# A backbone of three token mixers: all two-operand passes moved to VectorE, and a decay buffer of its own in the state-space stage

## The chip, the cores and the metric

The kernel runs on one core of one Trainium2 chip. The metric is the device time of one execution in microseconds (us). The engines are named as the profile names them: PE is TensorE (matmuls, with PEld for its weight loads), DVE is VectorE, ACT is ScalarE, POOL is GpSimd and SP is SyncE, which issues every DMA of this kernel.

## The reference, cut to what matters

Two layers over 256 context and 512 latent tokens of 1024 channels, all in float32. Each layer normalises and modulates the tokens, projects them into the inputs of three mixers, and projects the mixers' joined outputs back:

```python
for l in range(DEPTH):                      # DEPTH = 2
    u_lat = rmsnorm(h_lat, norm_w[l]) * (1.0 + scale[:, None]) + shift[:, None]
    ...
    ssd_c, ssd_l = ssd_branch(...)          # state space, 16 heads, chunks of 128 tokens
    gla_c, gla_l = gla_branch(...)          # gated linear attention, 4 heads, chunks of 64
    s5_c, s5_l = s5_branch(...)             # diagonal complex scan, 32 groups
    out_lat = jnp.concatenate([ssd_l, gla_l, s5_l], axis=-1) @ w_out[l]
    h_lat = h_lat + gate[:, None] * out_lat
return rmsnorm(h_lat, final_norm_w)
```

The state-space branch is the one that the change rewrites. With `acs` the running sum of the step sizes times a negative rate, it computes in each direction and chunk

```python
acs = jnp.cumsum(da, axis=-1)
decay = jnp.exp(segsum(da))                 # exp(acs[t] - acs[s]) for s <= t, else 0
cb = jnp.einsum("bclgn,bcsgn->bgcls", cm, bm)
y_diag = jnp.einsum("bgrcls,bcsgrp->bclgrp", cb[:, :, None] * decay, x)
decay_states = jnp.exp(acs[..., -1:] - acs)
states = jnp.einsum("bclgn,bgrcl,bclgrp->bcgrpn", bm, decay_states, x)
```

and adds what the state carried into the chunk contributes, decayed by exp(acs).

## The kernel before

A scheduler takes the instructions in the order of the program text and sets, by its own cost table, the order in which each engine executes them; each engine's queue is then fixed and in order. An instruction that waits holds everything behind it on its engine, and a DMA that waits on SP holds every later DMA.

Channels lie on the 128 partitions and tokens along the free dimension. Every matmul of a projection is done three times with a weight and an input split into a high and a low half: `wsplit` loads a weight (`wr`), ACT copies its high half (`wh`) and DVE subtracts (`wl`, line 413). `proj` (lines 489 and 491) does the input projections, lines 1023 and 1025 the S5 gate, and `out_part` (lines 1059 and 1061) the output projection. That comes in two parts of 8 blocks each: `spilled_part` needs the outputs of S5 and attention alone, the last part those of the state-space branch.

Passes with two operands are spread over DVE and POOL by hand:

- S5's output maps, `s5_out_map`: lines 375 and 380 to 385, seven POOL passes for each of 2 x 16 maps, on a block `cs` that is loaded for each (`in_s5cb`). The matmuls at line 394 use the result.
- The state-space stage, `ssd_parts`: for both groups of heads (g = 0 works in the tile `bA`, g = 1 in `bB`) and six steps, each step with three functions. `decay` loads the running sums of a chunk, repeated over all partitions (line 902, 1 MB, tensor `acsD`), forms cb and its two masked copies (`cbl` and `cbu`, lines 907 and 908), eight pairs of ACT and DVE passes for the exponents (line 913, in place in `rf`) and eight for the masked products (`q2`, line 915), then Exp and a product into `rf` (line 918). `within` multiplies by the tokens (line 923) and adds to `xy` (line 925). `between` does for both directions d: the state's contribution (lines 932 and 937), with its decay loaded by a DMA of 256 KB into `ep[d]` (line 934), the addition to `xy` on POOL (line 938), and the state's update (POOL at 941 and 951, PE at 943 and 946, DVE at 952).
- The attention stage (759, 762, 800, 830), one convolution tile of twelve (853 and 858), the sums of squares (`add_square`, 435), some splits (418) and some norms (452 and 1173).

POOL also does fills, copies of a few columns and the short recurrence of S5's powers (lines 625 to 629).

Of the kernel before, what the change touches and what calls it, by code (L numbers as in the profile page):

```python
# [36 lines left out]
POOL_CONV, POOL_NORM, POOL_FIN = (1,), (3, 5, 7), (0, 2, 4)  # L37
# [4 lines left out]
def hybrid_backbone_kernel(  # L42
# [36 lines left out]
    def cs(n=1024):  # L79
        return T("cs", [128, 1024], 3)[:, :n]  # L80
# [63 lines left out]
    GT = tri("GT", ALU.is_gt, -1, 1)  # L144
    LT = tri("LT", ALU.is_gt, 1, -1)
# [219 lines left out]
    def s5_out_map(l, bi, pw, buf):  # L365

        gs = 2 * bi
        w5, tmp, cb, cn = cuts(buf, 576, 288, 128, 32)
# [104 lines left out]
    def layer(l, u):  # L473
# [72 lines left out]
        for i, (lm, rhs) in enumerate(((LE, daf), (GE, dab), (GT, daf), (LT, dab))):  # L546
# [5 lines left out]
        act(wf.rearrange("p a b -> p (a b)"), pq[:, 192:384], AF.Exp)  # L552
# [190 lines left out]
        for hd in range(4):  # L743
# [513 lines left out]
```

## Time and profile before

| | us |
|---|---|
| median of 3 runs | 1688.12 |
| the 3 runs | 1688.12, 1677.69, 1688.44 |
| time of the profiled execution | 1689.88 |
| its span, first instruction to last | 1688.2 |
| PE busy in it | 1416.3 |
| DVE busy in it | 1169.3 |
| POOL busy in it | 598.7 |

A busy time is the union of an engine's instructions; a row "mean ns of one" is their duration from start to end, and neighbours on DVE overlap a little. "Idle before" is the time that an engine stood before those instructions, with what ended it. The chain of waits is followed back from the last instruction: at each step to what released it, or to the instruction ahead of it on its engine.

### The profile page before, as it was taken

What the parts mean: (1) busy time and instruction counts of PE and PEld (TensorE: products, weight loads), DVE (VectorE), ACT (ScalarE), POOL (GpSimd) and SP (SyncE); (2) the same over time, 40 slices, a digit from 0 to 9 for tenths busy, and PEclk for the clock granted to TensorE, in tenths of its full rate; (3) what the DMA queues carried; (4) which work ended last, traced back from release to release, by engine and by line L of the source; (5) the groups of instructions that cost most, each with busy time, mean ns of one, the idle gap of its engine ahead of it and who ended that gap; (6) DMA issues with size and microseconds to landing.
All of it is one profiled execution on the core that took longest, in us unless ns stands there. A gap on an engine that the chain in (4) does not pass through costs nothing.

```text
span 1688.2 us, 23555 instructions
## 1 busy us (share of the span) xinstructions
PE 1416.3 (84%) x8536; PEld 1145.0 (68%) x8536; DVE 1169.3 (69%) x2074; ACT 677.3 (40%) x1216; POOL 598.7 (35%) x634
## 2 busy tenths in 40 slices
PE   3777877999789688977778999997989897976896
PEld 1566656778777465765567786887779776754675
DVE  7867649988566872599787326369955696687863
ACT  3312213222634321765545124334355444545452
POOL 3403548623136671245432120042113110454332
PEclk9788888999798899997889999999989998997998
DMA  8565564332263426254365834542346242344542
GB/s 312 125 161 149 171 168 140 115 103 87 89 198 110 141 66 203 66 161 154 112 189 186 316 130 149 169 145 89 124 133 181 66 126 88 117 155 136 184 161 94
DMA packets 139885, 243.55 MB, mean 144 GB/s; under 512 B 31992, under 2 KB 72568, under 8 KB 139768
## 3 DMA queue, kind: packets, MB, share of 16 engines
q1 hardware_dynamic: 139768, 242.04, 46.4%
q8 instruction: 67, 1.10, 0.3%
q14 instruction: 50, 0.41, 0.1%
HBM read 192.81 MB, written 49.18 MB: 143 GB/s over the span
## 4 chain that ended last, share of the span: by engine, by line
PE 29%; DVE 14%; DMA 13%; ACT 5%; issue 4%; POOL 4%; SPq 1%; DVEq 0%; ACTq 0%; POOLq 0%
PE pl L489 8%; PE pl L1059 6%; DMA bB<-acsD 5%; DMA bA<-acsD 5%; PE pc L491 3%; DVE wl L413 3%; PE pc L1061 2%; ACT bB L121 1%; DVE xy L860 1%; PE pl L706 1%; ACT bA L121 1%; DVE bc L860 1%; DMA cs<-in_s5cb 1%; PE pa L204 1%; PE pl L1023 1%
## 5 line engine op out<-in xcount | busy, mean ns | idle before, releaser
L489 PE MATMUL pl<-hl,wh 128*128 128x512 f32 (+1 forms) x1184 | 407.3, 412 | 4.2 <-ACT wh L121 1.9
L489 PEld LDWEIGHTS pl<-hl,wh 128*128 128x128 f32 (+1 forms) x1184 | 225.3, 195 | 60.9 <-issue 7.2
L489 PE MATMUL pl<-hl,wl 128*128 128x512 f32 (+1 forms) x592 | 243.6, 412 | 14.0 <-DVE wl L413 14.0
L413 DVE TENSOR_TENSOR wl<-wr,wh 128x1024 fp32r<-128x1024 f32 (+1 forms) x122 | 168.2, 1379 | 98.3 <-ACT wh L121 97.4
L121 ACT ACTIVATE wh<-wr 128x1024 fp32r<-128x1024 f32 (+1 forms) x122 | 127.7, 1048 | 254.6 <-PE pc L491 79.4
L491 PE MATMUL pc<-hl,wh 128*128 128x256 f32 (+1 forms) x864 | 197.9, 305 | 2.6 <-ACT ev L121 1.2
L491 PEld LDWEIGHTS pc<-hl,wh 128*128 128x128 f32 (+1 forms) x864 | 152.3, 204 | 16.3 <-issue 5.0
L489 PEld LDWEIGHTS pl<-hl,wl 128*128 128x128 f32 (+1 forms) x592 | 114.4, 193 | 44.9 <-DVE wl L413 18.0
L491 PE MATMUL pc<-hl,wl 128*128 128x256 f32 (+1 forms) x432 | 129.1, 300 | 0.0
L1059 PE MATMUL pl<-hl,wh 128*128 128x512 f32 x256 | 92.8, 436 | 25.2 <-ACT cv L121 8.6
L491 PEld LDWEIGHTS pc<-hl,wl 128*128 128x128 f32 (+1 forms) x432 | 87.9, 204 | 3.5 <-issue 2.7
L121 ACT ACTIVATE ev<-pl 128x512 f32<-128x512 f32 (+1 forms) x96 | 51.2, 534 | 94.8 <-PE pl L706 31.0
L394 PE MATMUL pa<-cs 64*32 64x128 f32 x512 | 41.5, 303 | 53.6 <-POOL cs L382 23.2
L706 PE MATMUL pl<-wh,hl 128*128 128x256 f32 x384 | 80.4, 310 | 2.4 <-ACT ev L121 2.4
L375 POOL TENSOR_SCALAR cs<-cs 128x32 f32<-128x32 f32 x32 | 16.7, 523 | 181.6 <-DMA cs<-in_s5cb 94.7
L1059 PEld LDWEIGHTS pl<-hl,wh 128*128 128x128 f32 x256 | 51.5, 206 | 41.7 <-ACT cv L121 9.0
L121 ACT ACTIVATE bB<-bB 128x512 f32<-128x512 f32 (+4 forms) x40 | 45.6, 1140 | 79.3 <-DMA bB<-acsD 60.0
L706 PEld LDWEIGHTS pl<-wh,hl 128*128 128x128 f32 x384 | 67.1, 215 | 10.1 <-issue 4.8
L860 DVE SCALAR_TENSOR_TENSOR xy<-ev,par_sb,xy 128x256 f32<-128x256 f32 (+1 forms) x112 | 70.5, 672 | 0.7
L394 PEld LDWEIGHTS pa<-cs 64*32 64x32 f32 x512 | 21.2, 114 | 71.0 <-POOL cs L382 26.2
L706 PE MATMUL pl<-wl,hl 128*128 128x256 f32 x192 | 58.8, 309 | 1.8 <-DVE wl L413 1.8
L1023 PE MATMUL pl<-hl,wh 128*128 128x512 f32 x128 | 48.8, 456 | 11.2 <-ACT cv L121 11.0
(482 smaller groups left out, 3474.1 us busy)
## 6 DMA issues: line engine op xcount, KB each, us to landing
wr<-in_wblk SPq DMA_DIRECT2D x80, 512.0 KB
wr<-in_wout SPq DMA_DIRECT2D x32, 512.0 KB
hl<-in_mod_w SPq DMA_DIRECT2D x20, 512.0 KB
bA<-acsD SPq DMA_DIRECT2D x10, 1024.0 KB
bB<-acsD SPq DMA_DIRECT2D x10, 1024.0 KB
clD<-cs SPq DMA_DIRECT2D x64, 128.0 KB
cs<-clD SPq DMA_DIRECT2D x32, 256.0 KB
cs<-in_mod_w SPq DMA_DIRECT2D x16, 512.0 KB
```

Source lines behind the costliest of these rows:

```text
L121: return S.activation(out, in_, f, **kw)
L204: PE.matmul(pm[32 * q : 32 * q + 32], sc[:, k, :], w, start=k == 0, stop=k == 7)
L375: G.tensor_scalar(cn, cb[:, 0:32], -1.0, None, MUL)
L394: PE.matmul(pk[d][32 * gg : 32 * gg + 32], b0[64 * d : 64 * d + 64, a, :], w54[64 * d : 64 * d + 64, a, gg, d : 8 + d, :].rearrange("p k h ...
L413: V.tensor_tensor(wl, wr, wh.bitcast(F32), SUB)
L489: PE.matmul(p_l[:m], lhs, u[k][:, ui, LC:NT], start=st, stop=sp)
L491: PE.matmul(p_c[:m], lhs, u[k][:, ui, 0:LC], start=st, stop=sp)
L706: PE.matmul(p, u[k][:, ui, 128 * c : 128 * c + 128], ws[k // 4][wi][:, 256 * (k % 4) : 256 * (k % 4) + 256], start=n == 0, stop=n == 23)
L860: V.scalar_tensor_tensor(ac, raw[:, o + k : o + k + n], pcol("cw", w0 + k), ac, MUL, ADD)
L1023: PE.matmul(p_l, lhs, yg5[k][:, ui, LC:NT], start=n == 0, stop=n == 11)
L1059: PE.matmul(p_l, lhs, rhs[kk][:, ui, LC - t0 : NT - t0], start=st, stop=sp)
L1061: PE.matmul(p_c, lhs, rhs[kk][:, ui, 0:LC], start=st, stop=sp)
```

## The change

Every pass over two operands in SBUF that POOL did is done by DVE, the sums and splits included; `POOL_CONV`, `POOL_NORM` and `POOL_FIN` go. The negation at line 375 goes too: the last pass of a map has become one that negates and subtracts. Two masks (`GT`, `LT`) go, and the strict sums that they gave are made by subtracting `da` on DVE.

In the state-space stage the exponents get a buffer `ex` of their own, so `rf` and `rbw` are only read. To make room, the masked copies of cb stay in PSUM, beside cb in one bank, and `bt` becomes a small tile. The decay of direction 0 is computed from the rows that `decay` has loaded already (two Exp passes of 64 partitions), so that only direction 1 still loads `ep`. The product with it is written back to PSUM, and DVE adds it to `xy`.

```diff
-        G.tensor_scalar(cn, cb[:, 0:32], -1.0, None, MUL)
...
-        G.tensor_tensor(w54[:, 0], pr, cr, MUL)
...
+        V.tensor_tensor(w54[:, 0], pr, cr, MUL)
+        V.tensor_tensor(t54, pi, ci, MUL)
+        V.tensor_tensor(w54[:, 0], w54[:, 0], t54, SUB)
+        V.tensor_tensor(w54[:, 1], pi, cr, MUL)
+        V.tensor_tensor(t54, pr, ci, MUL)
+        V.scalar_tensor_tensor(w5[:, 288:576], w5[:, 288:576], -1.0, tmp, MUL, SUB)
...
-            eng.tensor_tensor(acc, acc, sq, ADD)
+            V.tensor_tensor(acc, acc, sq, ADD)
...
-            G.tensor_tensor(tmp, tmp, k, MUL)
+            V.tensor_tensor(tmp, tmp, k, MUL)
...
+            epb, xw, bt = wk[:, 5120:5632], wk[:, 5632:6144], bts[g]
...
-                pcb = pa(128)
...
-                V.tensor_tensor(cbl, pcb, LE, MUL)
-                V.tensor_tensor(cbu, pcb, GE, MUL)
+                pcb = pa(384)
+                cb, cbl, cbu = (pcb[:, 128 * j : 128 * j + 128] for j in range(3))
...
+                V.tensor_tensor(cbl, cb, LE, MUL)
+                V.tensor_tensor(cbu, cb, GE, MUL)
...
-                    act(rf[:, h, :], rf[:, h, :], AF.Identity, bias=naf[:, ih : ih + 1])
-                    V.scalar_tensor_tensor(rf[:, h, :], rbw[:, h, :], rb[:, ih : ih + 1], rf[:, h, :], SUB, MIN)
...
+                    act(ex[:, h, :], rf[:, h, :], AF.Identity, bias=naf[:, ih : ih + 1])
+                    V.scalar_tensor_tensor(ex[:, h, :], rbw[:, h, :], rb[:, ih : ih + 1], ex[:, h, :], SUB, MIN)
...
+                V.tensor_tensor(po, po, ep, MUL)
+                return po
+
+            def add(cc, p):
+                V.tensor_tensor(y_at(cc), y_at(cc), p.rearrange("p (t x) -> p t x", t=4), ADD)
...
-                        dma(ep[d], bass.AP(tensor=acsD[l].tensor, offset=acsD[l][cc, d, 8 * g].offset,
-                                           ap=[[512, 2], [0, 64], [1, 512]]))
-                        act(ep[d], ep[d], AF.Exp)
-                        V.tensor_tensor(ep[d], po, ep[d], MUL)
-                        G.tensor_tensor(y_at(cc), y_at(cc), ep[d].rearrange("p (t x) -> p t x", t=4), ADD)
+                    if reads[d]:
+                        if d == 0:
+
+                            ep = T("s5p", [128, 576], 1)[:, 0:512]
+                            for r in range(2):
+                                h_ = slice(64 * r, 64 * r + 64)
+                                act(ep[h_], wk[h_, 512 * r : 512 * r + 512], AF.Exp)
...
-                        G.tensor_tensor(heads(xw), heads(xtok(cc)), per_head(wv), MUL)
+                        V.tensor_tensor(heads(xw), heads(xtok(cc)), per_head(wv), MUL)
...
-                            G.tensor_tensor(heads(hs[d]), heads(hs[d]), per_head(dec[:, jd : jd + 8]), MUL)
+                            V.tensor_tensor(heads(hs[d]), heads(hs[d]), per_head(dec[:, jd : jd + 8]), MUL)
```

All line numbers from 902 on shift: the load of the decay rows is line 892 in the new text, that of `ep` line 943, `within`'s matmuls line 928, the state's contribution line 917, and its update lines 951 and 954. The scheduler orders the whole program anew, at three places as follows.

SP, in layer 0's state-space stage, before; L902 and L934 are the two loads of running sums, L410 a weight, L1030 the S5 gate, and the brackets name the engines waited for (DMAHW is a DMA queue's own count):

```order
L410 DMA wr_6944<-in_wout 128x1024 [waits DMAHW1_49,DVE_49,Activation_49]
L902 DMA bA_5138<-acsD_119 128x2x1024 [waits DMAHW2_49,PE_49]
L934 DMA bB_5139<-acsD_119 128x1x512 [waits DMAHW3_49,Pool_49]
L934 DMA bB_5139<-acsD_119 128x1x512 [waits DMAHW4_49,Pool_49]
L1030 DMA cv_6763<-sgD_111 128x768 [waits DMAHW5_49,Activation_49]
L902 DMA bB_5139<-acsD_119 128x2x1024 [waits DMAHW6_49,PE_49]
L963 DMA cs_6860<-zD_107 128x768 [waits DMAHW7_49]
L410 DMA wr_7004<-in_wout 128x1024 [waits DMAHW0_49,DVE_49]
```

Here a step's load (L902) and its two decay loads (L934) alternate, and each of the latter stands behind POOL. The same place on SP now (L892 and L943 are the loads of running sums, L406 a weight, L1039 the S5 gate):

```order
L892 DMA bB_5085<-acsD_115 128x2x1024 [waits DMAHW7_49,DVE_49,Activation_49]
L1039 DMA cv_6721<-sgD_107 128x768 [waits DVE_49]
L406 DMA wr_6962<-in_wout 128x1024 [waits DMAHW2_49,DMAHW1_49,DVE_49]
L943 DMA bA_5084<-acsD_115 128x1x512 [waits DVE_49]
L1039 DMA cv_6788<-sgD_107 128x768 [waits DMAHW3_49,Activation_49]
L406 DMA wr_7022<-in_wout 128x1024 [waits DMAHW6_49,DMAHW4_49,DVE_49]
L892 DMA bA_5084<-acsD_115 128x2x1024 [waits DMAHW5_49,DVE_49,Activation_49]
L943 DMA bB_5085<-acsD_115 128x1x512 [waits DVE_49]
```

The two loads waited for PE and POOL, and now L892 waits for DVE and ACT and L943 for DVE; for each step there is one L943 where there were two L934.

PE, at the end of layer 0's state-space stage, before; L932 is the state's contribution, L923 `within`, L1059 and L1061 the first part of the output projection (`hl` is one input's two halves):

```order
L932 MATMUL ps_6008<-bc_4500,bA_5138 128x128 x4
L1059 MATMUL pl_6950<-hl_6857,wh_6946 128x512
L1061 MATMUL pc_66<-hl_6857,wh_6946 128x256
L1059 MATMUL pl_6950<-hl_6857,wl_6947 128x512
L1061 MATMUL pc_66<-hl_6857,wl_6947 128x256
L1059 MATMUL pl_7010<-hl_6857,wh_7006 128x512
L1059 MATMUL pl_7010<-hl_6857,wl_7007 128x512
L932 MATMUL ps_6017<-bc_4500,bA_5138 128x128 x4
L923 MATMUL ps_6026<-bA_5138,m_433_4597 64x128 x8
L932 MATMUL ps_6036<-bc_4694,bB_5139 128x128 x4
L1059 MATMUL pl_7070<-hl_6636,wh_7066 128x512 x2
```

Here the projection's matmuls stand between those of the steps. The same place on PE now (L917 the contribution, L928 `within`, L954 and L951 the update, L897 cb, L1070 the last matmul of the first part of the output projection):

```order
L1070 MATMUL pc_66<-hl_6815,wl_7325 128x256
L951 MATMUL pa_5824<-ident,bc_4446 128x128
L954 MATMUL ps_5810<-bA_5084,bt_5086 128x512
L917 MATMUL ps_5816<-bc_4446,bA_5084 128x128 x4
L897 MATMUL pa_5842<-bc_4446 128x128
L951 MATMUL pa_5891<-ident,bc_4640 128x128
L954 MATMUL ps_5827<-bA_5084,bt_5086 128x512
L928 MATMUL ps_5831<-bA_5084,m_425_4543 64x128 x8
L951 MATMUL pa_5908<-ident,bc_4640 128x128
L917 MATMUL ps_5883<-bc_4640,bB_5085 128x128 x4
L954 MATMUL ps_5894<-bB_5085,bt_5087 128x512
L917 MATMUL ps_5900<-bc_4640,bB_5085 128x128 x4
```

The steps follow each other without the projection. Before, 74 of the 192 latent matmuls of that first part are issued ahead of the twelfth and last `within`, and the others after it; now all 192 are issued ahead of the ninth, and the last four steps stand with no projection between them.

POOL before, at two of layer 1's S5 output maps (`cs` is a map's block, `s5p` the powers):

```order
L375 TENSOR_SCALAR cs_2063<-cs_2063 128x32 [waits DMAHW6_49,DMAHW5_49,DMAHW7_49,DMAHW0_49,PE_49]
L380 TENSOR_TENSOR cs_2063<-s5p_1800,cs_2063 128x288
L381 TENSOR_TENSOR cs_2063<-s5p_1800,cs_2063 128x288
L383 TENSOR_TENSOR cs_2063<-s5p_1800,cs_2063 128x288 [waits Pool_49]
L375 TENSOR_SCALAR cs_2090<-cs_2090 128x32 [waits DMAHW2_49,DMAHW3_49,DMAHW1_49,PE_49]
L380 TENSOR_TENSOR cs_2090<-s5p_1800,cs_2090 128x288
L381 TENSOR_TENSOR cs_2090<-s5p_1800,cs_2090 128x288
```

Here POOL goes from one map to the next. DVE now, at one map (L848 is the convolution, L396 and L397 the small additions to a map, L409 a weight's low half):

```order
L396 TENSOR_TENSOR cs_2090<-cs_2090,pa_2101 64x16 [waits Activation_49]
L848 SCALAR_TENSOR_TENSOR bc_4640<-ev_4716,par_sb,bc_4640 128x512 [waits DVE_49]
L376 TENSOR_TENSOR cs_2142<-s5p_1778,cs_2142 128x288 [waits DMAHW5_49,DMAHW6_49,DMAHW4_49,DMAHW3_49]
L377 TENSOR_TENSOR cs_2142<-s5p_1778,cs_2142 128x288
L379 TENSOR_TENSOR cs_2142<-s5p_1778,cs_2142 128x288
L848 SCALAR_TENSOR_TENSOR bc_4640<-ev_4716,par_sb,bc_4640 128x256 [waits DVE_49]
L397 SCALAR_TENSOR_TENSOR cs_2090<-i_92,par_sb,cs_2090 64x16 [waits DVE_49]
L378 TENSOR_TENSOR cs_2142<-cs_2142 128x288 [waits DVE_49]
L409 TENSOR_TENSOR wl_4892<-wr_4889,wh_4891 128x1024 [waits PE_49,Activation_49]
L848 SCALAR_TENSOR_TENSOR bc_4640<-ev_4716,par_sb,bc_4640 128x256 [waits DVE_49]
L380 TENSOR_TENSOR cs_2142<-s5p_1778,cs_2142 128x288 [waits DVE_49]
```

The map's passes moved in between those of the convolution and the weights; its first pass waits for four to eight DMA counts, which POOL's did at L375 and DVE's does at L376.

## Rows read from the trace of the kernel before

**Rows 1.** The page, part 1: busy time, share of the span, instructions of each engine.
```profile
PE 1416.3 (84%) x8536; PEld 1145.0 (68%) x8536; DVE 1169.3 (69%) x2074; ACT 677.3 (40%) x1216; POOL 598.7 (35%) x634
```

**Rows 2.** The page, part 4: shares of the chain that ended last.
```profile
PE 29%; DVE 14%; DMA 13%; ACT 5%; issue 4%; POOL 4%; SPq 1%; DVEq 0%; ACTq 0%; POOLq 0%
...
PE pl L489 8%; PE pl L1059 6%; DMA bB<-acsD 5%; DMA bA<-acsD 5%; PE pc L491 3%; DVE wl L413 3%; PE pc L1061 2%; ACT bB L121 1%; DVE xy L860 1%; PE pl L706 1%; ACT bA L121 1%; DVE bc L860 1%; DMA cs<-in_s5cb 1%; PE pa L204 1%; PE pl L1023 1%
```

**Rows 3.** Busy time by stretch: start:end, length, engines (instructions), clock, DMA share, GB/s.
```profile
250.00:400.00 150.00, 131.91 (x835) 112.53 (x835) 131.69 (x209) 41.83 (x64) 83.62 (x78) 0.89 0.41 119
...
700.00:900.00 200.00, 157.75 (x911) 124.29 (x910) 161.05 (x277) 110.33 (x254) 86.06 (x62) 0.87 0.50 157
...
1450.00:1600.00 150.00, 117.90 (x595) 87.51 (x594) 124.50 (x216) 77.13 (x185) 74.30 (x54) 0.91 0.47 148
```

**Rows 4.** The low halves of the weights: all, those of 1050 to 1100, that stretch.
```profile
L413 DVE TENSOR_TENSOR wl<-wr,wh 128x1024 fp32r<-128x1024 f32 x120 | 166.8, 1390 | 98.2 <-ACT wh L121 97.4
...
L413 DVE TENSOR_TENSOR wl<-wr,wh 128x1024 fp32r<-128x1024 f32 x6 | 7.4, 1226 | 16.1 <-ACT wh L121 16.0
...
1050.00:1100.00 50.00, 49.75 (x311) 43.16 (x311) 19.37 (x40) 16.75 (x32) 0.00 (x0) 1.00 0.57 182
```

**Rows 5.** Timeline, DVE and then POOL: start, duration, instruction.
```profile
742.09 0.35 DVE L915 SCALAR_TENSOR_TENSOR bA<-bA,dts 128x128 f32<-128x128 f32 x1
...
742.35 0.68 DVE L925 TENSOR_TENSOR xy<-xy,ps 128x512 f32<-128x512 f32 x1
...
742.95 0.97 DVE L915 SCALAR_TENSOR_TENSOR bA<-bA,dts 128x128 f32<-128x128 f32 x1
...
742.71 1.06 POOL L951 TENSOR_TENSOR bB<-bB,dts 128x512 f32<-128x512 f32 x1 [2.23 <-PE ps L932]
```

**Rows 6.** Groups of DVE by line and shape: the decay's passes.
```profile
L913 DVE SCALAR_TENSOR_TENSOR bA<-bA,dts 128x128 f32<-128x128 f32 x80 | 37.9, 528 | 4.4 <-ACT bA L121 4.4
...
L913 DVE SCALAR_TENSOR_TENSOR bB<-bB,dts 128x128 f32<-128x128 f32 x80 | 32.6, 457 | 1.4 <-ACT bB L121 1.4
...
L915 DVE SCALAR_TENSOR_TENSOR bA<-bA,dts 128x128 f32<-128x128 f32 x80 | 35.2, 492 | 1.0 <-ACT bA L121 0.9
...
L915 DVE SCALAR_TENSOR_TENSOR bB<-bB,dts 128x128 f32<-128x128 f32 x80 | 35.3, 499 | 4.8 <-ACT bB L121 4.8
```

**Rows 7.** One line's instructions (minimum/median/maximum ns): a pass with one operand in PSUM.
```profile
L925 DVE TENSOR_TENSOR xy<-xy,ps x20: 672/676/682, 718.0 to 1598.5; 128x512 f32<-128x512 f32 x20
```

**Rows 8.** Groups of POOL by line and shape.
```profile
L380 POOL TENSOR_TENSOR cs<-s5p,cs 128x288 f32<-128x288 f32 x32 | 34.4, 1075 | 0.0
...
L941 POOL TENSOR_TENSOR bA<-m,wf 128x512 f32<-128x512 f32 x20 | 28.5, 1423 | 51.1 <-PE ps L946 38.7 <-ACT m L121 12.4
...
L938 POOL TENSOR_TENSOR xy<-xy,bA 128x512 f32<-128x512 f32 x18 | 28.4, 1581 | 32.4 <-DVE bA L937 32.3
...
L375 POOL TENSOR_SCALAR cs<-cs 128x32 f32<-128x32 f32 x32 | 16.7, 523 | 181.6 <-DMA cs<-in_s5cb 94.7 <-DVE bB L360 27.3 <-DMA gD<-cs 23.8
```

**Rows 9.** Groups of DVE: the nearest pass to those of the output maps.
```profile
L348 DVE TENSOR_TENSOR bA<-bA 64x288 f32<-64x288 f32 x2 | 0.9, 452 | 0.0
```

**Rows 10.** Who waited for the decay rows' loads: for L934, then for L902 (us, times).
```profile
  ACT bB L121: 60.0, 17
...
  ACT bA L121: 59.8, 18
...
  ACT bB L121: 17.5, 6
...
  ACT bA L121: 10.6, 8
```

**Rows 11.** Waits: SyncE's queue, TensorE, VectorE (us in total, times, longest).
```profile
SPq L934 <- POOL xy L938: 91.9, 26, 10.3
...
PE pa L394 <- POOL cs L382: 23.2, 7, 7.4
...
DVE bA L361 <- DMA bA<-in_s5b: 21.0, 6, 5.1
```

More of the change, by code (lines that the diff above doesn't have):

```diff
@@ L545, in layer @@
         pq = px(384)
-        for i, (lm, rhs) in enumerate(((LE, daf), (GE, dab), (GT, daf), (LT, dab))):
+        for i, (lm, rhs) in enumerate(((LE, daf), (GE, dab), (GE, daf), (LE, dab))):
             PE.matmul(pq[:, 96 * i : 96 * i + 96], lm, rhs, start=True, stop=True)
@@ L893, in ssd_parts @@
             xtok, bT, cT = xts[g], bcs[g][:, 0, :], bcs[g][:, 1, :]
-            rf, rbw, q2 = (wk[:, 1024 * j : 1024 * j + 1024].rearrange("p (h t) -> p h t", h=8) for j in range(3))
-            cbl, cbu = wk[:, 3072:3200], wk[:, 3200:3328]
-            hs = [wk[:, 3328 + 512 * d : 3840 + 512 * d] for d in range(2)]
-            ep = [wk[:, 4352 + 512 * d : 4864 + 512 * d] for d in range(2)]
-            xw, bt = wk[:, 5376:5888], wk[:, 5888:6016]
+            rf, rbw, ex, q2 = (wk[:, 1024 * j : 1024 * j + 1024].rearrange("p (h t) -> p h t", h=8) for j in range(4))
+            hs = [wk[:, 4096 + 512 * d : 4608 + 512 * d] for d in range(2)]
+            epb, xw, bt = wk[:, 5120:5632], wk[:, 5632:6144], bts[g]
             y_at = lambda c: xy[:, 4 * g : 4 * g + 4, 128 * c : 128 * c + 128]
+            reads = [i > 0 and not (last and cc < 2) for cc in (cf, cbk)]
+            inner = not (last and c < 2)
             def decay():
@@ L904, in decay @@
                             ap=[[0, 128], [2048, 2], [1, 1024]]))
-                pcb = pa(128)
-                PE.matmul(pcb, bT[:, 128 * c : 128 * c + 128], cT[:, 128 * c : 128 * c + 128], start=True, stop=True)
-                V.tensor_tensor(cbl, pcb, LE, MUL)
-                V.tensor_tensor(cbu, pcb, GE, MUL)
+                pcb = pa(384)
+                cb, cbl, cbu = (pcb[:, 128 * j : 128 * j + 128] for j in range(3))
+                PE.matmul(cb, bT[:, 128 * c : 128 * c + 128], cT[:, 128 * c : 128 * c + 128], start=True, stop=True)
+                V.tensor_tensor(cbl, cb, LE, MUL)
+                V.tensor_tensor(cbu, cb, GE, MUL)
                 for h in range(8):
@@ L950, in between @@
                             jd = 32 * cc + 16 * d + 8 * g
-                            G.tensor_tensor(heads(hs[d]), heads(hs[d]), per_head(dec[:, jd : jd + 8]), MUL)
+                            V.tensor_tensor(heads(hs[d]), heads(hs[d]), per_head(dec[:, jd : jd + 8]), MUL)
                             V.tensor_tensor(hs[d], hs[d], pst, ADD)
             none = lambda: None
-            return (none, none, between) if last and c < 2 else (decay, within, between)
+            return (decay, within, between) if inner else (none, none, between)
         def ssd_norm(g):
@@ L988, in layer @@
         wgs = [big("bA"), big("bB")]
+        bts = [T("bt", [128, 128], 2) for _ in range(2)]
         parts = [[ssd_parts(g, i) for i in range(6)] for g in range(2)]
@@ L1103, in layer @@
             if m < 7:
-                acc = add_square(acc, sq, hx2[:, m, t0:NT], G)
+                acc = add_square(acc, sq, hx2[:, m, t0:NT])
             else:
                 act(sq, hx2[:, m, t0:NT], AF.Square)
-            if last and m in POOL_FIN:
-                act(hx2[:, m, LC:NT], hx2[:, m, LC:NT], AF.Copy, scale=pcol("fnw", m))
             if m == 6:
```

92 lines of the change are left out of this document (40 added, 52 removed).

## Prediction

> **What bounds the kernel now.** I read the first part of the page first. PE is busy for 1416.3 us of 1688.2, DVE for 1169.3, POOL for 598.7 [rows 1]. No engine is full, so the question is what stands on the path that ends last, and the chain of waits answers it [rows 2]: PE 29%, DVE 14%, DMA 13%, ACT 5%, POOL 4%. Of the DMA share, 5% and 5% are loads of the repeated running sums `acsD` into `bB` and `bA`: some 165 us of the path lie in the state-space stage behind loads of data that is already on the chip or could be. The windows say where DVE, which is to take POOL's work, has room [rows 3]: in 250 to 400 us it is busy for 131.7 of 150 (S5 and convolution), in 700 to 900 for 161 of 200 and in 1450 to 1600 for 124.5 of 150 (both state-space stages). It is idle there for 18, 39 and 25.5 us.
>
> Then I asked whether DVE works at its own pace. The subtraction at line 413 takes 1390 ns over 120 instances, but 1226 in the stretch from 1050 to 1100, where POOL has no instruction [rows 4]. The timeline shows a single case: one L915 takes 0.35 us, the one beside POOL's L951 of 1.06 us takes 0.97 [rows 5]. The means of L913 and L915 (457 to 528 ns over 320 passes) are well above 350 [rows 6]. L925, with one operand in PSUM, is within 672 and 682 ns every time [rows 7]. So passes with two SBUF operands are stretched beside POOL's passes, and others are not.
>
> **Part 1, the stretched passes.** Line 413 loses 120 x 0.164 = 20 us. L913 and L915 have durations of 80 x (528 + 457 + 492 + 499) ns = 158 us, against 320 x 0.35 = 112: they lose 46. That is 66 us of 325, or 20%, in these lines alone. DVE's whole time at that rate would lose 240; passes with a PSUM operand lose nothing. The loss lies between 66 and 240; I take 150 (an estimate near the middle, since most of DVE's passes have two SBUF operands), 13% of DVE's 1169. On the chain DVE holds 14%, 236 us; 13% of it is **-30**, with 6% and 20% as bounds -13 to -48.
>
> **Part 2, POOL's own passes.** POOL holds 4% of the chain, 67.5 us. What does such a pass cost on DVE? Two rows bound it. A DVE pass of 128x512 takes 0.68 us and a POOL pass of that size beside it 1.06 [rows 5]: 0.64. The DVE pass nearest to those of the maps, 64x288, takes 452 ns against POOL's 1075 at L380 [rows 8, 9]: 0.42, too good, since POOL's row holds its own waits. I take 0.53, and another 0.88 because DVE's passes start closer than they last (742.35 to 742.95 for 0.68) [rows 5]: 0.47. On the chain this gives -36, say **-34** (bounds -20 to -50).
>
> The Trainium skill bears on that ratio (GPSIMD Engine Reference, section 3.1, Elementwise): it measures a two-input add at 4497 ns on GpSimd and 2293 on DVE, a ratio of 0.51 where the row's neighbours give 0.64. By it alone, as an estimate, the work that DVE takes over would be 235 us and not the 245 below; no step turns on it.
>
> **Part 3, what DVE takes over.** POOL's busy time is 598.7; 16.7 of it, the negation L375, vanishes [rows 8], and fills, small copies and the recurrence stay, for which I take a tenth, 60 (an estimate). The other 522 become 522 x 0.47 = 245 us of DVE (193 to 294 by the two ratios). DVE then needs 1169 - 150 + 245 = 1264 us, 75% of the span: not full on average. By stretch, with 13% off and POOL's busy time there x 0.47 on: 250 to 400 needs 115 + 39 = 154 of 150; 700 to 900 needs 140 + 40 = 180 of 200; 1450 to 1600 needs 109 + 35 = 144 of 150. So the S5 stretch becomes full and the state-space stages nearly so. DVE's other work stands behind these passes: the low halves `wl` that PE's projection waits for, the adds at L925. I price it at **+25**: 4 us over in the one stretch, some 20 for `wl` and L925 arriving later at PE where DVE has 6 to 20 us free instead of 25 to 39. Bounds 0 (all beside PE's work) to +60 (a quarter of the 245).
>
> **Part 4, the loads of the decay rows.** ACT waits 60.0 + 59.8 us for L934 and 17.5 + 10.6 for L902 [rows 10], 148 in all, 81% for L934. SP stands 91.9 us in front of L934 for POOL's L938, which frees the buffer [rows 8, 11]. Half of the L934 (direction 0) vanish. The other half go to a buffer that is freed by DVE's product in PSUM, without the 1.5 us of L938 behind it. L902 no longer waits for `within` on PE. So about 40% of the 165 us of the chain, 66, could go. But DVE is the next late engine: after part 3 it has 20 + 6 us idle in those two stretches, and up to 45 if the passes there are stretched by the 20% of L913 and L915. The gain is capped at 45; I take half, **-23** (0 to -45).
>
> **Part 5, the S5 output maps.** POOL's L375 stands idle for 181.6 us over the 32 maps, of which 94.7 for the load `in_s5cb` and 23.8 for the store `gD` [rows 8]. Nothing on POOL minded. The first pass of a map now stands at DVE's head with those DMA counts, and behind it are the convolution and `wl`. Seven passes before, six now. PE's wait for POOL in front of L394, 23.2 us [rows 11], gets shorter, as a map takes some 2.7 us (six at 452 ns) instead of up to 7.0 (six at 1075 and one at 523) [rows 8, 9]. The scheduler places a map between other DVE passes, and a DVE that comes to a map later than POOL did finds more of its loads landed. I take 1 us a map, half of it uncovered: **+15** (0 to +95, the whole of the waits for `in_s5cb`). For comparison, DVE loses 21.0 us in six waits for the S5 inputs today [rows 11], 3.5 us each.
>
> **Part 6, order.** The projection that filled PE beside the last state-space steps is now issued ahead of the ninth `within`, and four steps and the norm run bare. In exchange the steps before them have more cover. I take **0**; the rows do not price it, and -20 to +30 is about a fifth, either way, of the 8% of the chain (135 us) that L1059 and L1061 hold [rows 2]. The masked copies of cb hold a PSUM bank for eight passes; the other bank carries on, and I price that at 0, with up to 20 decays x 8 x 0.35 = 56 us if nothing covers it; this is inside the bound of part 3. The sums of squares, splits and norms moved to DVE are in the 245; ACT works beside them.
>
> **The sum** is made against the profiled execution's 1689.88 us: -30 - 34 + 25 - 23 + 15 + 0 = -47, so 1643. That execution lies 1.8 above the median of the three runs, so the forecast is **1641**.
>
> **Rivals.** (a) *The loads vanish fully from the chain*: if DVE has more room than I think (the stretch is nearer 240 than 150), parts 1 and 4 give -48 and -66, and DVE's added work costs nothing: -48 - 34 - 66 + 0 + 15 = -133, or 1555; halfway between that and the forecast stands about 1600, which I give as its time. For: 10% of the chain is `acsD`. Against: DVE's 144 of 150.
>
> (b) *DVE becomes the bound* and the gains of parts 1 and 2 are eaten by the longer queue. Then parts 3 and 4 stand at +60 and 0: -30 - 34 + 60 + 0 + 15 = +11, to -13 if the maps' waits are covered and PE's cover is better: 1675 to 1699, no difference that can be told. For: 154 of 150 in the S5 stretch [rows 3]. Against: PE waits for POOL's slow passes there now. A rule of the Trainium skill points this way (Perfetto Trace Analysis, section Optimizing Scalar/DVE Operations): a saturated DVE may be relieved by Scalar or even GpSimd, but these passes share a read port, so moving between DVE and GpSimd might not help. That the two stop each other agrees with the 0.97 us of L915 beside L951; that a move gains nothing is open until the change runs.
>
> (c) *Slower: DVE stands for the maps' loads.* The 94.7 us of POOL's waits for `in_s5cb` become waits of DVE in the stretch where it is already full. The other parts sum to -62, so the point from which it decides is 62 / 32 = 1.9 us of exposed wait a map; today's is 3.0. With all of it: 1688.1 - 62 + 94.7 = 1721. For: the queue is in order, and L361's six waits show 3.5 us for such loads. Against: the loads are small, and a DVE that is later finds them landed.
>
> (d) *The change does not do what it says*: the stretch comes from something other than POOL (DMA writes, say). DVE then needs 1169 + 245 = 1414 us, 84% like PE, and the sum loses part 1 and takes part 3's upper end: about 1705 to 1715. The stretch without POOL instructions and L925 speak against it.
>
> **How the numbers follow.** About 1% is what a measurement of this kernel can tell from no change. The forecast (1610 to 1671) gets 0.50, (a) 0.15, (b) 0.18, (c) 0.13, (d) 0.04. Faster by over 1% are the forecast and (a): 0.65; same (b): 0.18; slower (c) and (d): 0.17. For the range, the half widths of the six terms (18, 15, 30, 23, 48, 25), added as squares, give 70 around 1641: 1571 to 1711; I shift it by a little to hold more of (c), **1575 to 1718**. The forecast's own range is 1610 to 1671.
>
> **What would show it.** Part 1: L413 near 1226 ns, the passes of L913 and L915 near 350, everywhere. Part 2: no POOL on the chain. Part 3: DVE busy near 1260 and above 145 in the S5 stretch. Part 4: `acsD` at less than 5% of the chain together, ACT's waits for the loads under 60 us. Part 5: the first pass of the maps with DVE's idle time for `in_s5cb` below 32 us. Part 6: PE's idle time in the last four steps of each state-space stage. I would be wrong with the size if DVE stays stretched, and with the sign if the waits for `in_s5cb` on DVE pass 60 us.

## The result, and the profile after

The changed kernel takes 1658.26 us (median of 4 runs, 1652.08 to 1663.01) against 1683.12 before: a ratio of 0.985, 95% interval 0.982 to 0.988. That is 25 us, or 1.5%, less; 47 were forecast. The profiled execution's span is 1661.3 us.

The page of the changed kernel, parts 1 and 4 (busy times, then the chain by engine and by line), against [rows 1, 2]:

```profile
PE 1394.5 (84%) x8536; PEld 1129.3 (68%) x8536; DVE 1215.7 (73%) x2487; ACT 676.6 (41%) x1209; POOL 62.2 (4%) x192
...
PE 45%; DVE 23%; DMA 20%; ACT 7%; issue 5%; SPq 1%; DVEq 0%; ACTq 0%
...
PE pl L480 15%; PE pl L1068 6%; PE pc L482 6%; DMA bB<-acsD 5%; DMA bA<-acsD 4%; DMA bc<-lpD 3%; ACT bA L120 2%; PE pc L1070 2%; DMA blD<-bA 2%; PE pl L700 2%; DVE wl L409 2%; DMA gD<-cs 2%; PE ps L954 1%; ACT bB L120 1%; PE pa L201 1%
```

POOL is at 62 us and off the chain. DVE is busy for 46 us more, not 95 more. The loads of running sums still hold 9% of the chain (5% and 4%), where under 5% was forecast. Both pages give shares of the whole span, but the chain of before could be followed back only to 508 us, and its shares in [rows 2] sum to 70%; that of the changed kernel reaches back to the start. So POOL's 4% and DVE's 14% leave out layer 0's S5 maps and all that lies ahead of them, while both state-space stages are in.

Groups of DVE by line and shape in the changed kernel, against [rows 4, 6, 9]:

```profile
L409 DVE TENSOR_TENSOR wl<-wr,wh 128x1024 fp32r<-128x1024 f32 x120 | 146.8, 1224 | 62.2 <-ACT wh L120 59.5 <-PE pc L482 2.1
...
L904 DVE SCALAR_TENSOR_TENSOR bB<-pa,dts,bB 128x128 f32<-128x128 f32 x80 | 27.6, 346 | 18.4 <-ACT bB L120 18.4
...
L908 DVE SCALAR_TENSOR_TENSOR bA<-bA,dts 128x128 f32<-128x128 f32 x80 | 24.0, 346 | 17.6 <-ACT bA L120 17.6
...
L376 DVE TENSOR_TENSOR cs<-s5p,cs 128x288 f32<-128x288 f32 x32 | 14.4, 451 | 12.2 <-DMA cs<-in_s5cb 10.7 <-DMA clD<-cs 1.5
```

The low halves take 1224 ns where they took 1390, and the passes of the decay (L904 and L908, once L915 and L913) 346 where they took 457 to 528. Summed over all DVE instructions, the time above the tenth percentile of each line and shape was 186 us before and is 20 now. So nearly all of the stretch is gone. The maps' passes take 451 ns, and the first of each (L376) waited 10.7 us in all for `in_s5cb`. But see the third column of L904: DVE now stands idle in front of it, for ACT. I come back to that.

Busy time by stretch in the changed kernel, the three of [rows 3]:

```profile
250.00:400.00 150.00, 124.68 (x793) 105.84 (x793) 137.43 (x235) 39.05 (x58) 22.50 (x44) 0.90 0.44 126
700.00:900.00 200.00, 154.91 (x918) 120.73 (x916) 152.34 (x307) 89.77 (x208) 0.00 (x0) 0.85 0.53 175
1450.00:1600.00 150.00, 106.66 (x496) 77.49 (x497) 114.01 (x224) 72.87 (x157) 0.00 (x0) 0.81 0.40 126
```

No stretch of DVE is full. To see where PE stood, I cut both programs at the same places: the end of layer 0's S5 maps, the end of layer 0's projection, the start and the end of layer 1's projection. Windows of the kernel before (length, then PE, PEld, DVE, ACT, POOL):

```profile
0.00:285.00 285.00, 205.14 (x1341) 160.28 (x1343) 199.04 (x464) 81.95 (x153) 123.57 (x142) 0.84 0.61 178
285.00:714.00 429.00, 371.18 (x2419) 307.61 (x2417) 298.74 (x512) 159.40 (x273) 186.42 (x236) 0.92 0.40 117
714.00:1032.00 318.00, 266.90 (x1583) 209.40 (x1582) 212.63 (x335) 140.25 (x283) 112.23 (x74) 0.90 0.53 178
1032.00:1473.00 441.00, 407.75 (x2416) 342.66 (x2417) 309.19 (x536) 194.90 (x311) 86.42 (x124) 0.94 0.41 124
1473.00:1688.20 215.20, 165.29 (x783) 125.08 (x782) 149.67 (x230) 100.82 (x198) 90.08 (x60) 0.90 0.44 144
```

and of the changed kernel:

```profile
0.00:256.00 256.00, 195.32 (x1383) 154.73 (x1385) 184.98 (x556) 78.54 (x146) 4.51 (x18) 0.89 0.63 183
256.00:671.00 415.00, 354.61 (x2376) 293.77 (x2370) 326.78 (x649) 154.82 (x259) 25.27 (x88) 0.91 0.46 136
671.00:994.00 323.00, 264.36 (x1587) 207.05 (x1585) 224.62 (x418) 148.78 (x300) 2.03 (x3) 0.89 0.49 161
994.00:1421.00 427.00, 404.60 (x2398) 343.63 (x2399) 310.93 (x557) 186.62 (x290) 30.36 (x83) 0.94 0.42 128
1421.00:1661.30 240.30, 175.64 (x802) 130.14 (x800) 168.37 (x310) 107.89 (x216) 0.00 (x0) 0.85 0.38 121
```

Length minus PE's busy time is PE's idle time: before 79.9, 57.8, 51.1, 33.3 and 49.9; now 60.7, 60.4, 58.6, 22.4 and 64.7. By length, the first two stretches give 43 us and layer 1's projection 14; the two stretches that hold the state-space stages take back 5 and 25. So the change pays in the first stage, for its length much less where PE is busy for 87% to 95% anyway, and something in the state-space stage eats a part. (Over the whole span PE's idle time is only 5 us less, 267 after 272, and its busy time 22 us less with the same instructions; the ends of its matmuls are modelled, and I don't take that apart.)

Who waited for the loads of direction 1's decay in the changed kernel (us, times), against [rows 10]:

```profile
  ACT bA L120: 49.6, 9
  ACT bB L120: 40.0, 9
```

ACT waits 89.6 us for them, where it waited 119.8 for the loads of both directions; under 60 was forecast.

### The profile page after: what moved, and what is told of

Same layout as the page of the kernel before. It is cut to its first block, busy times and chain, and to the rows that moved or that the text cites. A ratio compares the mean times of both kernels' runs of the same rounds, so it can differ in the third digit from the quotient of the medians.

```text
span 1661.3 us, 23247 instructions
## 1 busy us (share of the span) xinstructions
PE 1394.5 (84%) x8536; PEld 1129.3 (68%) x8536; DVE 1215.7 (73%) x2487; ACT 676.6 (41%) x1209; POOL 62.2 (4%) x192
## 4 chain that ended last, share of the span: by engine, by line
PE 45%; DVE 23%; DMA 20%; ACT 7%; issue 5%; SPq 1%; DVEq 0%; ACTq 0%
PE pl L480 15%; PE pl L1068 6%; PE pc L482 6%; DMA bB<-acsD 5%; DMA bA<-acsD 4%; DMA bc<-lpD 3%; ACT bA L120 2%; PE pc L1070 2%; DMA blD<-bA 2%; PE pl L700 2%; DVE wl L409 2%; DMA gD<-cs 2%; PE ps L954 1%; ACT bB L120 1%; PE pa L201 1%
## 5 line engine op out<-in xcount | busy, mean ns | idle before, releaser
L480 PE MATMUL pl<-hl,wh 128*128 128x512 f32 (+1 forms) x1184 | 403.2, 409 | 2.0 <-ACT hl L120 0.8
L480 PE MATMUL pl<-hl,wl 128*128 128x512 f32 (+1 forms) x592 | 242.3, 410 | 22.4 <-DVE wl L409 22.2
L120 ACT ACTIVATE wh<-wr 128x1024 fp32r<-128x1024 f32 (+1 forms) x122 | 127.7, 1050 | 286.0 <-PE pc L482 117.3
L409 DVE TENSOR_TENSOR wl<-wr,wh 128x1024 fp32r<-128x1024 f32 (+1 forms) x122 | 148.1, 1215 | 62.2 <-ACT wh L120 59.5
L1068 PE MATMUL pl<-hl,wh 128*128 128x512 f32 x256 | 91.2, 426 | 9.1 <-ACT hl L120 4.8
L700 PE MATMUL pl<-wh,hl 128*128 128x256 f32 x384 | 74.8, 293 | 2.4 <-ACT ev L120 2.4
L848 DVE SCALAR_TENSOR_TENSOR xy<-ev,par_sb,xy 128x256 f32<-128x256 f32 (+1 forms) x128 | 73.6, 611 | 0.5
L700 PEld LDWEIGHTS pl<-wh,hl 128*128 128x128 f32 x384 | 61.5, 197 | 7.8 <-ACT ev L120 3.6
L120 ACT ACTIVATE bB<-bB 128x1024 f32<-128x1024 f32 (+4 forms) x31 | 40.0, 1292 | 61.7 <-DMA bB<-acsD 40.0
L1068 PE MATMUL pl<-bA,wh 128*128 128x512 f32 x128 | 45.1, 426 | 10.1 <-ACT bA L120 7.5
L1068 PE MATMUL pl<-hl,wl 128*128 128x512 f32 x128 | 53.0, 416 | 0.2 <-DVE wl L409 0.2
L1032 PE MATMUL pl<-hl,wh 128*128 128x512 f32 x128 | 43.8, 417 | 10.1 <-DVE cv L1045 5.5
```

The lines of the kernel that those rows point to most:

```text
L120: return S.activation(out, in_, f, **kw)
L409: V.tensor_tensor(wl, wr, wh.bitcast(F32), SUB)
L480: PE.matmul(p_l[:m], lhs, u[k][:, ui, LC:NT], start=st, stop=sp)
L700: PE.matmul(p, u[k][:, ui, 128 * c : 128 * c + 128], ws[k // 4][wi][:, 256 * (k % 4) : 256 * (k % 4) + 256], start=n == 0, stop=n == 23)
L848: V.scalar_tensor_tensor(ac, raw[:, o + k : o + k + n], pcol("cw", w0 + k), ac, MUL, ADD)
L1032: PE.matmul(p_l, lhs, yg5[k][:, ui, LC:NT], start=n == 0, stop=n == 11)
```

## The experiments

Each is one edit, timed in three rounds beside the kernel before (1681.3, 1682.3 and 1682.8 us in the three groups). Theory A: the moves carry the gain. Theory B: the rewrite of the state-space stage does.

**e1, the moves without the rewrite.** `ssd_parts` is that of before, with VectorE in it (the strict sums stay as in the changed kernel):

```diff
-            G.tensor_tensor(...)    # lines 938, 941, 951 of before
+            V.tensor_tensor(...)
```

> The state-space stage as it was before the change, but with its POOL passes on DVE too; all other moves as in the changed kernel. Theory A (the gain comes from the moves: DVE's two-operand passes are no longer stretched, POOL's slow passes leave the chain; the rewrite of the state-space stage adds little): 1645 to 1665 us, L413's successor near 1215 ns, stretch gone. Theory B (the gain comes from the state-space rewrite, that is from fewer loads of running sums; the moves by themselves only trade POOL time for DVE time): 1680 to 1695.

1656.4 us, ratio 0.985 (0.981 to 0.989): all of the gain. Theory A holds. Cut at the same places, e1's stretches are 256, 428, 315, 440 and 222 us long: against before, 29 us less in the first, 1 to 3 less in the next three and 7 more in the last. So the moves gain in the first stretch, and nothing in sum behind it.

**e2, the rewrite without the moves.** The new `ssd_parts` and the new strict sums in the kernel before, the token and state products on POOL.

```diff
+            rf, rbw, ex, q2 = (...)
+                pcb = pa(384)
...
+                        G.tensor_tensor(heads(xw), heads(xtok(cc)), per_head(wv), MUL)
```

> The rewrite of the state-space stage alone (buffer ex, masked products in PSUM, direction 0 from the loaded rows, product written back to PSUM and added by DVE; the strict sums by subtraction, which free the room), every other POOL pass left on POOL, the stage's token and state products too. Theory A: 1675 to 1690, low halves still at about 1390 ns. Theory B: 1655 to 1668.

1683.0 us, ratio 1.000 (0.997 to 1.003). The rewrite is worth nothing by itself.

**e3, the S5 maps back on POOL.**

```diff
-        V.tensor_tensor(w54[:, 0], pr, cr, MUL)
+        G.tensor_tensor(w54[:, 0], pr, cr, MUL)
```

(and so for the other passes of a map, with the negation at line 375).

> The changed kernel with the S5 output maps back on POOL. If the moves pay by ending the stretch and by shorter maps (theory A): slower than the changed kernel by 8 to 20 us, about 1668 to 1678, DVE passes beside the maps stretched again. If the maps' waits for their loads at the head of DVE's queue cost what they may (the rival of the prediction): faster by 10 or more, 1650 or less. If both are small: within 5 us.

1667.5 us, ratio 0.992 (0.988 to 0.995): 9 us slower than the changed kernel. TensorE's waits in e3 (us in total, times, longest):

```profile
PE pa L391 <- POOL cs L379: 19.3, 9, 5.8
...
PE pa L391 <- POOL cs L382: 18.8, 10, 5.1
```

PE waits for the maps again; for L379's pass (L382 before) that was 23.2 us in [rows 11]. In the changed kernel the same two passes, now on DVE, keep PE waiting for 3.4 us:

```profile
PE pa L390 <- DVE cs L378: 2.4, 1, 2.4
...
PE pa L390 <- DVE cs L381: 1.0, 1, 1.0
```

The move of the maps gains; it doesn't cost. But it isn't what shortens the first stretch: layer 0's maps end at 258 us in e3, at 256 in the changed kernel and at 285 before.

**e4, the projection spread over the last steps.** The first matmul of block m is ordered on PE behind one of the last eight `within`:

```diff
-                p_c, p_l = out_part(m, k0, rhs, order)
+                p_c, p_l = out_part(m, k0, rhs, order, wins[len(wins) - 8 + m])
```

> The changed kernel with the first matmul of each of the eight blocks of the first part of the output projection ordered on PE behind one of the last eight within (one block a step), in both layers, so that the last steps of the state-space stage have projection beside them. Theory A1 (the bare steps at the end cost the 26 us by which the last 240 us of layer 1 are longer than before): 12 to 25 us faster than the changed kernel, 1635 to 1646. Theory A2 (the steps are paced by the loads of direction 1's decay and by DVE and ACT, the fill only changes place): within 5 us of it, 1653 to 1663, or slower.

1661.0 us, ratio 0.987 (0.983 to 0.992): no difference. The bare steps are not what costs; A1 falls.

**e6, without the loads of direction 1's decay.**

```diff
-                            dma(ep, bass.AP(... offset=acsD[l][cc, 1, 8 * g].offset, ...))
-                            act(ep, ep, AF.Exp)
+                            for r in range(2):
+                                h_ = slice(64 * r, 64 * r + 64)
+                                act(ep[h_], wk[h_, 1024 + 512 * r : 1536 + 512 * r], AF.Exp)
```

> The changed kernel without the loads of direction 1's decay: it takes the Exp of direction 1's rows of the chunk that decay has loaded, which is the wrong chunk for direction 1, with the same passes otherwise. Theory C1 (the loads pace the steps, and the steps set the end; the removed loads of direction 0 bought nothing because those of direction 1 run at the same time and still have to land): 15 to 40 us faster than the changed kernel, 1618 to 1643, acsD off the chain. Theory C2 (the steps have slack, because the projection fills PE beside them and DVE and ACT pace them): within 6 us of it, 1652 to 1664.

1595.2 us, ratio 0.948 (0.943 to 0.953): 63 us less than the changed kernel, more than C1 gave. With the masked copies in PSUM, these loads set the pace of the steps, and the steps do set the end. So the loads that the change removed ought to be worth something too, and the next runs look for what the rewrite loses elsewhere.

**e8, the masked copies in SBUF and direction 0's decay in place.**

```diff
-                pcb = pa(384)
-                cb, cbl, cbu = (pcb[:, 128 * j : 128 * j + 128] for j in range(3))
+                cb = pa(128)
+                cbl, cbu = cbs[:, 256 * g : 256 * g + 128], cbs[:, 256 * g + 128 : 256 * g + 256]
...
-                            ep = T("s5p", [128, 576], 1)[:, 0:512]
+                                ep = wk[h_, 512 * r : 512 * r + 512]
+                                act(ep, ep, AF.Exp)
```

> The changed kernel with the masked copies of cb in SBUF (in the tile s5p) instead of PSUM, and direction 0's decay formed in place in rf instead of in the one tile s5p that both groups share. Theory D1 (the rewrite lengthens the loop of steps, 208 and 144 us against 187 and 111 without it, because the masked copies hold one of two PSUM buffers and both groups queue for one tile): the loops 15 to 30 us shorter and the kernel 5 to 15 us faster, 1643 to 1653. Theory D2 (the loops are longer because they begin earlier and share PE with more projection): within 5 us, loops as long.

1627.4 us, ratio 0.967 (0.963 to 0.971): 31 us less than the changed kernel, more than D1 gave. D2 falls. Two halves tell which edit it was. (In place, the two halves of the partitions lie in different columns of `rf`, so that DVE multiplies direction 0's contribution in two passes of 64 partitions instead of one; that holds for e9, e10 and e11 too.)

**e9, only direction 0's decay in place** (the second hunk of e8).

> The changed kernel with direction 0's decay formed in place in rf, the masked copies left in PSUM: one half of e8, which took 31 us off the changed kernel. Theory E1 (the cost was that both groups queue for the one tile s5p, a step's exponents of the one behind the product of the other): 1625 to 1638. Theory E2 (the cost was the masked copies, which hold one of the two PSUM buffers of the transposes and of cb over 16 passes): within 6 us of the changed kernel, 1652 to 1664. Both by half: about 1642.

1678.2 us, ratio 0.998 (0.995 to 1.000): 20 us slower than the changed kernel. Both theories gave a gain or nothing; neither foresaw a loss. SyncE's waits in e9 have a row that the changed kernel's don't:

```profile
SPq L892 <- DVE ps L921: 69.9, 10, 15.7
```

L892, the load of the next step's decay rows, now waits for L921, the product that still reads them in `rf`. The shared tile `s5p` was not the cost; it set `rf` free early. How much of the 20 us is this wait and how much the second pass for each of these products (DVE is busy for 1230.6 us, 15 more) was not measured apart.

**e12, only the masked copies in SBUF**, in the last two heads of `ex`, which are written last:

```diff
-                pcb = pa(384)
-                cb, cbl, cbu = (pcb[:, 128 * j : 128 * j + 128] for j in range(3))
+                cb = pa(128)
+                cbl, cbu = ex[:, 6, :], ex[:, 7, :]
```

> The other half of e8: the masked copies in SBUF (in the last two heads of ex, which are written last), direction 0's decay in the shared tile s5p as in the changed kernel. E1: 1652 to 1664. E2: 1625 to 1638.

1604.8 us, ratio 0.954 (0.951 to 0.957): 53 us less than the changed kernel: a version that beats both. E2 holds, with a larger size than it gave. Parts 1 and 4 of its page:

```profile
PE 1382.7 (86%) x8536; PEld 1117.3 (70%) x8536; DVE 1210.1 (76%) x2487; ACT 676.4 (42%) x1209; POOL 61.9 (4%) x192
...
PE 38%; DVE 27%; DMA 22%; ACT 7%; issue 5%; SPq 1%; DVEq 0%; ACTq 0%
...
PE pl L480 13%; PE pl L1068 6%; DMA bA<-acsD 5%; PE pc L482 5%; DMA bB<-acsD 4%; DMA bc<-lpD 3%; DMA gD<-cs 3%; ACT bA L120 3%; DVE wl L409 2%; PE pc L1070 2%; DMA blD<-bA 2%; PE pl L700 2%; ACT bB L120 1%; PE pa L390 1%; DVE ps L919 1%
```

Cut at the same places, e12's stretches are 256, 414, 292, 418 and 221 us long. Of the 60 us between the two profiled executions, 50 lie in the two stretches that hold the state-space stages (31 and 19). TensorE's mean granted clock there is 0.96 and 0.90, against 0.89 and 0.85 in the changed kernel (between its two levels, 1.2 and 2.4 GHz), and 11 of the 50 us are PE's busy time, the others its idle time. The order changes too: in layer 0 the scheduler now spreads the first part of the output projection over the steps, with 158 of its 192 latent matmuls ahead of the twelfth `within`, where the changed kernel has all of them ahead of the ninth. That alone is not the gain: e4 spreads them much alike (163 ahead of the twelfth) with the masks in PSUM, and gains nothing.

How the masks cost it is seen at L904. Of the changed kernel, who kept L904 waiting (first two rows) and who waited for it (us, times):

```profile
  ACT bA L120: 18.4, 15
  ACT bB L120: 18.4, 20
  ACT bB L120: 28.7, 30
  ACT bA L120: 19.9, 21
  PE pa L201: 12.5, 1
```

and of e12 (the first row kept it waiting):

```profile
  ACT bA L120: 1.3, 2
  ACT bA L120: 3.6, 3
  ACT bB L120: 2.2, 4
```

With the masks in PSUM, DVE and ACT wait for each other: 36.8 us on DVE for ACT, 48.6 on ACT for DVE; in SBUF it is 1.3 and 5.8. The order shows why. Of the changed kernel, ACT's passes over one masked copy, one of each group:

```
L120 ACTIVATE bB_5085<-pa_5254,dts_609 128x128 [waits DVE_49]
L120 ACTIVATE bA_5084<-pa_5191,dts_609 128x128 [waits DVE_49]
```

and of e12:

```
L120 ACTIVATE bA_5084<-bA_5084,dts_609 128x128 x7
```

Both copies lie in one bank, one is read by ACT and the other by DVE, and each of ACT's passes is made to wait for DVE's pass before it. In SBUF seven go in a row without a wait. The timeline of the changed kernel, ACT and then DVE (start, duration):

```profile
815.85 0.37 ACT L120 ACTIVATE bA<-pa,dts 128x128 f32<-128x128 f32 x1 [0.90 <-DVE pa L899]
...
818.70 0.37 ACT L120 ACTIVATE bA<-pa,dts 128x128 f32<-128x128 f32 x1 [0.38 <-DVE bA L904]
...
821.96 0.37 ACT L120 ACTIVATE bA<-pa,dts 128x128 f32<-128x128 f32 x1 [2.72 <-DVE bA L904]
...
815.53 0.29 DVE L899 TENSOR_TENSOR pa<-pa,GE 128x128 f32<-128x128 f32 x1
...
818.33 0.34 DVE L904 SCALAR_TENSOR_TENSOR bA<-pa,dts,bA 128x128 f32<-128x128 f32 x1
...
821.59 0.34 DVE L904 SCALAR_TENSOR_TENSOR bA<-pa,dts,bA 128x128 f32<-128x128 f32 x1
```

From the first of these ACT passes to the third it is 6.1 us, since between two turns DVE works off other passes of 0.7 to 1.2 us that stand in its queue. From cb's matmul to the last L904 the bank is held for 28 us on average (20 decays, 566 us in sum), and there are two such banks: one wait of PE for it is the 12.5 us at L201 above. In e12 the bank is held until the second masked copy is made, 13 us on average. `within` of group 1, first and last start, in layer 0 and in layer 1, first in e1:

```profile
L911 PE MATMUL ps<-bB,cs x96: 272/273/473, 685.9 to 865.5; 128*64 128x128 f32 x96
...
L911 PE MATMUL ps<-bB,cs x64: 272/284/476, 1471.6 to 1563.6; 128*64 128x128 f32 x64
```

then in the changed kernel:

```profile
L928 PE MATMUL ps<-bB,cs x96: 272/273/476, 684.3 to 887.2; 128*64 128x128 f32 x96
...
L928 PE MATMUL ps<-bB,cs x64: 272/273/476, 1465.9 to 1584.0; 128*64 128x128 f32 x64
```

then in e12:

```profile
L928 PE MATMUL ps<-bB,cs x96: 272/273/477, 681.5 to 849.4; 128*64 128x128 f32 x96
...
L928 PE MATMUL ps<-bB,cs x64: 272/273/476, 1417.9 to 1511.3; 128*64 128x128 f32 x64
```

From the first to the last it is 180 and 92 us without the rewrite, 203 and 118 with it, 168 and 93 with the masks in SBUF.

**e10, a third buffer for direction 1's decay** (e8 with the masks in `ex`, the free `s5p` as the third, taken in turn):

```diff
-                            ep = epb
+                            ep = eps[nep[0] % 3]
+                            nep[0] += 1
```

> e8 with the masked copies in the last two heads of ex, and the tile s5p, free now, as a third buffer of direction 1's decay, the three taken in turn by both groups. Theory C1 (these loads pace the steps; the kernel without them took 1595): a third buffer lets a load start earlier, 1600 to 1620. Rival (a load starts late because SP's queue is in order and it stands behind the load of the decay rows, whatever buffer is free): within 6 us of e8, 1621 to 1633.

1639.6 us, ratio 0.975 (0.971 to 0.979): 12 us slower than e8, 35 slower than e12, which has its masks in the same place. Both ranges missed.

**e11, its loads ahead in the text**: each is written before the next step's `decay`.

```diff
+                    parts[g][i + 1][3]()
                     parts[g][i + 1][0]()
```

> e10 with the text of each of these loads moved ahead of the load of the next step's decay rows. C1: 1598 to 1615, below e10. Rival: as e10, since most of these loads still stand right behind a load of decay rows in SP's queue.

1650.7 us, ratio 0.981 (0.978 to 0.984): slower again, and outside both ranges. So a third buffer taken in turn by both groups gains nothing here. What does hold these loads was not settled; both versions have the in-place decay that cost 20 us in e9.

**e7, needless POOL passes**, on the kernel of e1:

```diff
         V.tensor_tensor(wl, wr, wh.bitcast(F32), SUB)
+        for q in range(6):
+            G.tensor_tensor(junk[:, 0:128], wl[:, 128 * (q % 4) : 128 * (q % 4) + 128].bitcast(F32), LE, MUL)
```

> The kernel of e1 (moves only) with six needless POOL passes of 128x128 with two SBUF operands behind each of the 120 weight splits, writing a tile that nothing reads. It prices contention with DVE by itself, spread over the projections. Theory A: DVE's passes are stretched again (L409's successor above 1300 ns) and the kernel is 8 to 25 us slower than e1, 1664 to 1681. Rival (in the projections DVE's stretch stands beside PE's work and costs nothing; the gain came from POOL's slow passes leaving the path): stretched again, but within 5 us of e1's 1656.

1691.4 us, ratio 1.004 (1.001 to 1.007): 35 us slower than e1, more than theory A gave; L410 itself stays at 1238 ns, where theory A wanted over 1300, since the passes start behind it. Part 1 of e1's page:

```profile
PE 1409.5 (85%) x8536; PEld 1143.6 (69%) x8536; DVE 1214.4 (73%) x2487; ACT 663.9 (40%) x1191; POOL 61.7 (4%) x192
```

and of e7's, with POOL's needless passes (minimum, median and maximum ns):

```profile
PE 1405.2 (84%) x8536; PEld 1136.0 (68%) x8536; DVE 1288.6 (77%) x2487; ACT 662.9 (39%) x1191; POOL 590.4 (35%) x924
...
L412 POOL TENSOR_TENSOR junk<-wl,LE x732: 453/466/12976, 44.3 to 1661.7; 128x128 f32<-128x128 f32 x183
```

DVE has the same instructions and is busy for 74 us more.

**e7b, the control**: one such pass and twelve fills.

```diff
+        G.tensor_tensor(junk[:, 0:128], wl[:, 0:128].bitcast(F32), LE, MUL)
+        for q in range(12):
+            G.memset(junk[:, 0:256], 0.0)
```

> The same as e7, but with one such pass and twelve POOL fills of 128x256, which read nothing, behind each weight split: the control for the order and for the hold on the weight's low half. Both theories: within 5 us of e1, L409's successor at 1215 to 1260 ns.

1662.2 us, ratio 0.987 (0.982 to 0.993), 6 us above e1, just outside the 5 that were given, with POOL busy for 649 us. It is POOL's reading beside DVE that costs, not its being busy. (e7's passes also hold the low half's tile some us longer; the one wait for that in e7's trace is 2.9 us.)

## Why the prediction came out as it did

**Parts 1, 2, 3 and 5, the moves: right in sum, open in the split.** They came to -30, -34, +25 and +15, or -24; e1 measures 1656.4 against 1681.3, or -25. Part 1's stretch did vanish, 166 us of it (150 estimated), and e7 shows that POOL's reading beside DVE costs time by itself: 74 us of DVE's busy time and 35 us of the kernel's. Part 3 took DVE to 1264 us and full in the S5 stretch; it is 1216 and 137 of 150. Part 5's +15 was too much: DVE's waits for `in_s5cb` are 10.7 us, where 1 us a map was taken, half of it uncovered, and e3 makes the maps' move worth -9 as a whole, with its shares of parts 1 to 3. Part 2, with POOL off the chain, was not tested apart from these.

That -24 meets -25 is partly luck. The shares were read from a chain that goes back only to 508 us, and e1 has its gain in the first 256. Neither the maps on POOL (e3, 258 us) nor POOL's reading passes (e7, 256; most of its loss lies in layer 0's projection) bring the 29 us back; e2, which has the new strict sums but not the moves, ends that stretch at 276. Which of the other passes gave the rest no run tells.

**Part 4, the loads: undersized, and hidden.** It took -23 with a bound of -45. The rewrite with the masks in SBUF against no rewrite (e12 against e1) is -52, past the bound, and e6 prices the loads that are left at 63 (with the masks in PSUM; no run has both edits, so the two need not add). The step that failed is the cap: DVE was thought to be next, with 20 and 6 us free in the two stretches of the state-space stage; it is idle there for 48 and 36. How much of the 52 is direction 0's loads, how much the buffer `ex` and the sum from PSUM, no run tells.

**Part 6, the masked copies: the step that failed.** It says "the other bank carries on, and I price that at 0", on a hold of 8 x 0.35 us a decay. The hold is 28 us, because ACT and DVE take turns over one bank and each turn stands in two queues. It costs 53 us (the changed kernel against e12). That the prediction names 56 as the most it could cost is chance: they came from a hold of 2.8 us. With part 4's 52 it cancels, so the rewrite as made gives 0 (e2), and the change 25 us where 47 were forecast. The time lies in the forecast's own range (1610 to 1671) because these two errors stand against each other. Whether the turns or the held bank cost more is open: e12 ends the one and shortens the other.

The rest of part 6 was right at 0: the bare steps that the order shows cost nothing (e4), and of the 25 us by which layer 1's last stretch is longer, 19 are gone in e12.

**The rivals.** (a), the loads vanishing from the chain, didn't happen: `acsD` holds 9% of it. That e12 takes 1605, near the 1600 given for (a), is not its confirmation, for there too `acsD` holds 5% and 4%. (b) and (c) fall by DVE's windows and by L376's 10.7 us; (d) by L409's 1224 ns. The Trainium skill's remark beside (b), that moving operations between DVE and GpSimd might not help (Perfetto Trace Analysis, section Optimizing Scalar/DVE Operations), leaves the question open; for this kernel and this direction e1 answers it, with 25 us gained.

## What to carry to other kernels

- A move of two-operand passes from GpSimd to VectorE is priced by what VectorE loses beside GpSimd too, not by the passes alone; and it need not pay in every stage: here the gain lay in the first 256 us of 1661.
- An operand in PSUM that two engines read over many small passes can cost more than the passes, as here: look at the waits in front of each pass in the order, and price the hold by the queues that stand between two turns, not by the passes' durations.
- When a change of several parts moves the time little, undo each part alone: here a gain of 52 us and a loss of 53 lay in one function.

## What the runs showed of the hardware

The loss goes both ways. In e7 POOL's pass of 128x128 takes 0.466 us at the median, but the longest takes 12.98 and all 732 together 531 us, not the 341 of the median; the longest one, at 546.6 us, stands beside 30 DVE passes that follow each other without a gap, and ends 0.3 us after the last of them. DVE's sum of `xy` and a PSUM tile of 128x512 takes 0.68 us at the median in every kernel here, e7 included (0.67 to 0.72 each).
